# Loading the input norm's weights by themselves, and casting the first two weight pieces in halves

## The chip, the cores and the metric

The kernel runs on one core of a Trainium2 chip. The metric is the device time of one execution in microseconds (us). Before the change the median of three runs is 1170.52 us (1168.86 to 1172.1).

Engines are named as in the profile: PE is the matrix engine (PEld its weight loads), DVE the vector engine, ACT the scalar engine, POOL the general engine, SP the engine that issues most DMAs. A name with q (SPq, ACTq) is the issuing side of an engine. L12 is line 12 of the kernel's file.

## The reference, cut to what matters

One decoder layer on 256 tokens of width 2048, in float32:

```python
h = rms_norm(x, attn_norm_g)          # x * rsqrt(mean(x*x)) * attn_norm_g
proj = h @ w_in                       # 2048 x 4448
shifted = token_shift(proj[..., :RWKV_SHIFT_DIM], rwkv_mu)
y = concat(rwkv7_mixer(split(shifted), ...), mla_mixer(split(proj rest), ...))
x = x + y @ w_out
h = rms_norm(x, ffn_norm_g)
x = x + (silu(causal_conv3(h @ w_gate) + conv_b) * (h @ w_up)) @ w_down
return rms_norm(x, final_norm_g)
```

The change touches only how `x * attn_norm_g` and the first columns of `w_in` get onto the chip.

## The kernel before, in words

Every product is made of float32r halves: a value is split into `hi` (the value rounded by a cast) and `lo` (what the rounding lost), and a product is three matmuls, hi·hi, hi·lo and lo·hi. Weights come in pieces of 128 partitions x 1024 floats (512 KB). `piece` (L125) issues one DMA on SP into one of three `raw` buffers (`NRAW` is 3), casts it to `hi` on ACT (L133) and subtracts on DVE for `lo` (L134). A `raw` buffer comes free when its `lo` is done, so SP, which issues in order, waits there, and everything behind waits too.

The input is loaded transposed, in four tiles `xT` of 128 x 1024 (four 128-row blocks of 256 tokens each). `xsplit` (L137) multiplies each block by its 128 norm weights, held as one column per block, with ACT for `hi` (L143) and DVE for `lo` (L144). The norm's own factor, one over the root mean square of a token, is applied behind the product; its sums come from a second, token-major copy of `x` (tiles `xt`, L323, squared and summed on ACT, L324).

All per-channel vectors of the layer are packed in one array `vec` (128 x 283): its first 16 columns are the weights of the input norm, the other 267 are shift factors, decay offsets, convolution weights and the like. A second array `cst` (128 x 388) holds an identity, masks and the rope frequencies. Both are loaded from ACT's queue, `vec` at L122 before anything else, `cst` at L330, which stands behind the third input tile in the code and ends up at the head of ACT's queue.

The start runs as follows. PE does 20 matmuls of ones by ones (L297 and L298, each recorded as two passes), which depend on nothing but a memset. In the meantime SP loads xT tile 0, the first half of column tile 0 (`win[0, 0]`, rows 0 to 1023 of the input product), the first half of column tile 25, xT tiles 1 and 2, the second halves of column tiles 0 and 25, and xT tile 3. The loop at L327 then makes both column tiles together, four blocks at a time. After them come the positions (`rposi`, L338), column tile 26, two `xt` tiles, column tile 1, two more `xt` tiles, column tiles 2 and 3, and all the others.

What sets the order: on SP the code order is kept by hand; on the other engines a scheduler orders the instructions by its own estimate of when their data come. Every engine then works strictly in that order. From the end of the input projection on, PE's order is a list written out by hand.

Of the kernel before, what the change touches and what calls it, by code (L numbers as in the profile page):

```python
# [9 lines left out]
F32 = mybir.dt.float32  # L10
F32R = mybir.dt.float32r
BF16 = mybir.dt.bfloat16  # L12
I32 = mybir.dt.int32
AF = mybir.ActivationFunctionType
ALU = mybir.AluOpType
AX = mybir.AxisListType

P = 128
# [36 lines left out]
def hybrid_layer(ctx: ExitStack, tc: tile.TileContext, a: dict, out: bass.AP):  # L55
    nc = tc.nc
    V, S, PE = nc.vector, nc.scalar, nc.tensor
    PSUM = bass.MemoryType.PSUM

    sb = ctx.enter_context(tc.tile_pool(name="sb", bufs=1))  # L60
# [5 lines left out]
    def nm(s):  # L66
        uid[0] += 1
        return f"{s}{uid[0]}"

    NT2, NAT, NS4, NRAW, NHI, NLO, NMM, NCH, NT1 = 3, 2, 21, 3, 3, 3, 3, 3, 5  # L70

    def s4(dt=F32, n="s4"):
        return sb.tile([P, 1024], dt, tag="s4", name=nm(n), bufs=NS4)
# [8 lines left out]
    def hl4(slot, n, off=0):  # L82
        return a8(slot, n, off=off).rearrange("p (k s) t -> p k s t", s=2)
# [19 lines left out]
    def con(shape, n, dt=F32):  # L103
        return sb.tile(shape, dt, name=n, bufs=1)
# [3 lines left out]
    xT = a["xT"]  # L108
    xs_ = [hl4(g, "x") for g in range(4)]
    pad2 = con([P, 24], "pad2")  # L110
    nc.gpsimd.memset(pad2, 0.0)
    vec = con([P, NVEC], "vec")
    cst = con([P, NCST], "cst")

    def vv(name, i, rows=slice(0, P)):
        return vec[rows, VOFF[name] + i:VOFF[name] + i + 1]
# [2 lines left out]
    gmask = cst[:, C_MK:C_MK + P]  # L119
    blk2 = cst[:, C_BLK:C_BLK + 2]  # L120

    nc.scalar.dma_start(vec, a["vec"])  # L122


    def piece(src, dst=None, off=0):  # L125
        raw = sb.tile([P, 1024], F32, tag="raw", name=nm("raw"), bufs=NRAW)
        last_w[0] = nc.sync.dma_start(raw, src).ins
        if dst is None:
            hi = sb.tile([P, 1088], F32R, tag="hi", name=nm("hi"), bufs=NHI)[:, off:off + 1024]
            lo = sb.tile([P, 1088], F32R, tag="lo", name=nm("lo"), bufs=NLO)[:, off:off + 1024]  # L130
        else:
            hi, lo = (dst.rearrange("p k t -> p (k t)")[:, q * 1024:(q + 1) * 1024] for q in range(2))
        S.copy(hi, raw)  # L133
        last_lo[0] = V.tensor_tensor(lo, raw, hi.bitcast(F32), ALU.subtract).ins  # L134
        return hi, lo

    def xsplit(g):  # L137
        raw = s4(n="xraw").rearrange("p (k t) -> p k t", k=4)
        nc.sync.dma_start(raw, xT[:, g * 4:(g + 1) * 4, :])
        for j in range(4):  # L140
            k = g * 4 + j
            h = xs_[g][:, j, 0, :]
            S.activation(h, raw[:, j, :], AF.Copy, scale=vv("ag", k))  # L143
            last_x[0] = V.scalar_tensor_tensor(xs_[g][:, j, 1, :], raw[:, j, :], vv("ag", k),  # L144
                                               h.bitcast(F32), ALU.mult, ALU.subtract).ins
        return raw

    last_w, last_lo, last_x = [None], [None], [None]
# [11 lines left out]
    def prod_c(acc, pieces, act, kt0, n, first, last):  # L160
        hi, lo = pieces
        for j in range(n):
            for s in range(2):
                PE.matmul(acc[:, :T], hi[:, j * P:(j + 1) * P], act(kt0 + j)[:, s, :],  # L164
                          start=first and j == 0 and s == 0, stop=False)
        for j in range(n):
            i = PE.matmul(acc[:, :T], lo[:, j * P:(j + 1) * P], act(kt0 + j)[:, 0, :], start=False,  # L167
                          stop=last and j == n - 1)
        return i.ins
# [24 lines left out]
    def in_tile(i, pf=mm):  # L194
        acc = pf()
        for h in range(2):
            prod_c(acc, piece(a["win"][i, h]), x_hl, h * 8, 8, h == 0, h == 1)
        flush()
        return acc

    def rsqrt(src, scale, eps, w, eng=None, part=None):

        e = eng or nc.gpsimd
        m, y, t = st("rm", w), st("ry", w), st("rt", w)
        if part is None:
            e.tensor_scalar(m, src, 0.5 * scale, 0.5 * eps, ALU.mult, ALU.add)
        else:
            e.tensor_scalar(part, part, 0.5 * scale, 0.5 * eps, ALU.mult, ALU.add)
            e.tensor_scalar(m, src, 0.5 * scale, part, ALU.mult, ALU.add)
        e.tensor_scalar(y.bitcast(I32), m.bitcast(I32), -0.5, float(0x5f3759df - 2 ** 22 - 2 ** 31), ALU.mult, ALU.add)  # L210
        for _ in range(3):
            if e is V and w == 1:
                V.scalar_tensor_tensor(t, y, m, y, ALU.mult, ALU.mult)
            else:
                e.tensor_tensor(t, y, y, ALU.mult)
                e.tensor_tensor(t, t, m, ALU.mult)
            if e is V:
                V.scalar_tensor_tensor(y, t, -1.5, y, ALU.add, ALU.mult)
            else:
                e.tensor_scalar(t, t, -1.5, None, ALU.add)  # L220
                e.tensor_tensor(y, y, t, ALU.mult)
        return y


    def bcast(rs, dst, pf=ch, tf=t1):
        pb = pf("rsb")
        for tb in range(2):
            dg = tf("dg", P)
            V.tensor_scalar(dg, ident, rs[:, tb:tb + 1], None, ALU.mult)
            PE.matmul(pb[:, tb * P:(tb + 1) * P], ones, dg, start=True, stop=True)  # L230
        return V.tensor_copy(dst, pb[:, :T]).ins
# [83 lines left out]
    pcs = {}  # L315
    wt0 = (0, 25, 26)
    ssx = st("ssx", 4)
    kacc = {}

    def sums(h):  # L320
        for tb in range(2):
            t, o = s4(n="xt"), h * 2 + tb
            nc.sync.dma_start(t, a["x"][tb * P:(tb + 1) * P, h * 1024:(h + 1) * 1024])  # L323
            S.activation(t, t, AF.Square, accum_out=ssx[:, o:o + 1])  # L324

    with tc.manual_schedule(engines={mybir.EngineType.SP}):
        for g in range(4):  # L327
            xsplit(g)
            if g == 2:
                nc.scalar.dma_start(cst, a["cst"])  # L330
            if g % 2 == 0:
                for i in range(2):
                    pcs[i, g // 2] = piece(a["win"][wt0[i], g // 2])
            for i in range(2):
                hl = tuple(u[:, (g % 2) * 512:(g % 2 + 1) * 512] for u in pcs[i, g // 2])
                prod_c(acc0[i], hl, x_hl, g * 4, 4, g == 0, g == 3)
        posi = s4(n="rposi")[:, 0:T]
        nc.sync.dma_start(posi.bitcast(I32), a["pos"].broadcast_to([P, T]))  # L338
        for h in range(2):
            prod_c(acc0[2], piece(a["win"][26, h]), x_hl, h * 8, 8, h == 0, h == 1)  # L340
        sums(0)
        kacc[0] = in_tile(1)
        dve0 = last_lo[0]
        sums(1)
        kacc[1] = in_tile(2, at)
        rsB = sb.tile([P, T], F32, tag="rsB", name="rsB", bufs=1)
        nc.gpsimd.tensor_tensor(ssx[:, 0:2], ssx[:, 0:2], ssx[:, 2:4], ALU.add)
        rs1 = con([P, 2], "rs1")
        nc.gpsimd.tensor_copy(rs1, rsqrt(ssx[:, 0:2], 1.0 / DM, EPS, 2))
        bcast(rs1, rsB)  # L350
        kacc[2] = in_tile(3, ch)
        rope_tables()
        lora = s4(n="lora")
        nc.sync.dma_start(lora, a["lora"])
# [26 lines left out]
    def shifted(acc, i, rows=slice(0, P), dst=None):  # L381
        h = hbuf()[:, 1:258]
        scaled(h[rows, 1:257], acc, rsB, rows)
        o = t1("sh") if dst is None else dst
        S.activation(o[rows], h[rows, 1:257], AF.Copy, scale=om_mu[rows, i:i + 1])
        V.scalar_tensor_tensor(o[rows], h[rows, 0:256], vv("mu", i, rows), o[rows], ALU.mult, ALU.add)
        return o
# [74 lines left out]
    for p in range(8):  # L462
        pp, g = p // 2, p % 2
# [4 lines left out]
        k = shifted(acc, 1 + p)  # L468
# [44 lines left out]
    for p in range(8):  # L513
        pp, g = p // 2, p % 2
# [261 lines left out]
    bufs = {}  # L776
# [390 lines left out]
    for blk, nf in enumerate(NFS):  # L1167
# [11 lines left out]
        n = nf // 2  # L1179
        held = []  # L1180
        for c in range(4):
            accs = [mm() for _ in range(2)]
            for i in range(n - (4 if blk == 1 and c == 3 else 0)):
                prod_a(accs, piece(a["wdn"][c, f0 // 2 + i]), h_hi, h_lo, i * 2, 2, i == 0, i == n - 1)
                if blk == 1 and i == 2:
                    q = n - 4 + c
# [98 lines left out]
```

## Time and profile before

| | us |
|---|---|
| three runs, median (lowest to highest) | 1170.52 (1168.86 to 1172.1) |
| profiled execution, its own time | 1171.28 |
| span of its trace, first to last instruction | 1169.3 |
| PE busy | 1151.5 (98%) |
| DVE busy | 807.0 (69%) |
| ACT busy | 610.0 (52%) |

The profile's page covers one execution. Busy times are unions of instruction times; a matmul's recorded time includes its passage through the array, so that a PE shown as busy can still be streaming slower than it could. The idle time before an instruction is listed with what released it.

### The profile page before, as it was taken

What the parts mean: (1) busy time and instruction counts of PE and PEld (TensorE: products, weight loads), DVE (VectorE), ACT (ScalarE), POOL (GpSimd) and SP (SyncE); (2) the same over time, 40 slices, a digit from 0 to 9 for tenths busy, and PEclk for the clock granted to TensorE, in tenths of its full rate; (3) what the DMA queues carried; (4) which work ended last, traced back from release to release, by engine and by line L of the source; (5) the groups of instructions that cost most, each with busy time, mean ns of one, the idle gap of its engine ahead of it and who ended that gap; (6) DMA issues with size and microseconds to landing.
All of it is one profiled execution on the core that took longest, in us unless ns stands there. A gap on an engine that the chain in (4) does not pass through costs nothing.

```text
span 1169.3 us, 19472 instructions
## 1 busy us (share of the span) xinstructions
PE 1151.5 (98%) x7669; PEld 1018.2 (87%) x7669; DVE 807.0 (69%) x1333; ACT 610.0 (52%) x912; POOL 18.5 (2%) x45
## 2 busy tenths in 40 slices
PE   9999999999999999999999999999999999999996
PEld 9899999999878888888888888888888888888885
DVE  6897669746997577777767774544677777775653
ACT  6884346445653465555555553333455555554441
POOL 1200000000000000000000000000000000000000
PEclk9999999999999999999999999999999999999999
DMA  9645456715635555555555655665555565576672
GB/s 329 198 142 166 136 166 199 216 46 163 194 126 178 193 175 175 197 184 196 194 191 192 197 189 190 197 190 192 195 198 190 189 198 185 194 234 199 209 216 79
DMA packets 71227, 216.24 MB, mean 185 GB/s; under 512 B 17648, under 2 KB 18032, under 8 KB 71136
## 3 DMA queue, kind: packets, MB, share of 16 engines
q1 hardware_dynamic: 70208, 212.89, 56.2%
q10 hardware_dynamic: 576, 1.39, 0.4%
q8 instruction: 60, 0.98, 0.4%
q0 software_dynamic: 352, 0.72, 0.3%
q14 instruction: 31, 0.25, 0.1%
HBM read 210.85 MB, written 3.41 MB: 183 GB/s over the span
## 4 chain that ended last, share of the span: by engine, by line
PE 88%; DMA 4%; DVE 3%; ACT 2%; issue 1%; SPq 1%; ACTq 0%; DVEq 0%
PE mm L1080 27%; PE mm L1091 14%; PE mm L808 8%; PE mm L189 7%; PE mm L187 7%; PE mm L188 7%; PE mm L164 5%; PE mm L793 3%; PE mm L167 3%; PE mm L867 2%; DVE lo L134 1%; PE px L686 1%; PE pg L542 1%; DMA raw<-in_win 1%; PE py L686 1%
## 5 line engine op out<-in xcount | busy, mean ns | idle before, releaser
L134 DVE TENSOR_TENSOR lo<-raw,hi 128x1024 fp32r<-128x1024 f32 x376 | 459.8, 1223 | 269.2 <-ACT hi L133 198.9
L133 ACT CAST hi<-raw 128x1024 fp32r<-128x1024 f32 x376 | 395.7, 1053 | 422.5 <-PE mm L1080 126.1
L1080 PE MATMUL mm<-z,hi 128*128 128x512 f32 x1408 | 351.7, 392 | 0.8 <-DVE z L1032 0.8
L1080 PEld LDWEIGHTS mm<-z,hi 128*128 128x128 f32 x1408 | 251.5, 188 | 44.3 <-DVE z L1032 1.2
L1091 PEld LDWEIGHTS mm<-z,lo 128*128 128x128 f32 x1408 | 186.4, 188 | 14.9
L1091 PE MATMUL mm<-z,lo 128*128 128x256 f32 x1408 | 189.1, 276 | 0.0
L189 PE MATMUL mm<-hi,hl 128*128 128x512 f32 x336 | 130.7, 389 | 0.0
L188 PE MATMUL mm<-lo,hh 128*128 128x512 f32 x336 | 130.7, 389 | 0.0
L187 PE MATMUL mm<-hi,hh 128*128 128x512 f32 x336 | 119.7, 389 | 0.0
L164 PE MATMUL mm<-x,hi 128*128 128x256 f32 x768 | 103.0, 282 | 0.2 <-ACT hi L133 0.2
L164 PEld LDWEIGHTS mm<-x,hi 128*128 128x128 f32 x768 | 93.8, 188 | 2.0 <-ACT hi L133 0.4
L189 PEld LDWEIGHTS mm<-hi,hl 128*128 128x128 f32 x336 | 63.1, 188 | 13.2
L188 PEld LDWEIGHTS mm<-lo,hh 128*128 128x128 f32 x336 | 63.1, 188 | 13.1
L187 PEld LDWEIGHTS mm<-hi,hh 128*128 128x128 f32 x336 | 63.0, 188 | 12.9
L167 PE MATMUL mm<-x,lo 128*128 128x256 f32 x384 | 55.3, 281 | 0.0
L808 PE MATMUL mm<-hi,yhi 128*128 128x512 f32 x128 | 50.7, 396 | 0.0
L808 PE MATMUL mm<-lo,yhi 128*128 128x512 f32 x128 | 50.5, 395 | 0.0
L808 PE MATMUL mm<-hi,ylo 128*128 128x512 f32 x128 | 50.3, 393 | 0.0
L167 PEld LDWEIGHTS mm<-x,lo 128*128 128x128 f32 x384 | 48.8, 188 | 1.1 <-issue 1.0
L793 PE MATMUL mm<-x,hi 128*128 128x256 f32 x256 | 34.6, 286 | 0.0
L793 PEld LDWEIGHTS mm<-x,hi 128*128 128x128 f32 x256 | 31.6, 192 | 0.7
L808 PEld LDWEIGHTS mm<-hi,ylo 128*128 128x128 f32 x128 | 24.1, 188 | 5.3 <-DVE ylo L965 0.4
(294 smaller groups left out, 1120.6 us busy)
## 6 DMA issues: line engine op xcount, KB each, us to landing
raw<-in_wgu SPq DMA_DIRECT2D x176, 512.0 KB, 3.3
raw<-in_wdn SPq DMA_DIRECT2D x88, 512.0 KB, 4.2
raw<-in_win SPq DMA_DIRECT2D x70, 512.0 KB, 3.9
raw<-in_wout SPq DMA_DIRECT2D x32, 512.0 KB, 3.3
raw<-in_wuq SPq DMA_DIRECT2D x6, 512.0 KB, 4.4
xraw<-in_xT SPq DMA_DIRECT2D x4, 512.0 KB, 6.1
xt<-in_x SPq DMA_DIRECT2D x4, 512.0 KB, 7.5
raw<-in_wuv SPq DMA_DIRECT2D x4, 512.0 KB, 4.8
```

What stands on the lines that cost most here:

```text
L133: S.copy(hi, raw)
L134: last_lo[0] = V.tensor_tensor(lo, raw, hi.bitcast(F32), ALU.subtract).ins
L164: PE.matmul(acc[:, :T], hi[:, j * P:(j + 1) * P], act(kt0 + j)[:, s, :], start=first and j == 0 and s == 0, stop=False)
L167: i = PE.matmul(acc[:, :T], lo[:, j * P:(j + 1) * P], act(kt0 + j)[:, 0, :], start=False, stop=last and j == n - 1)
L187: PE.matmul(accs[tb], ah, wh, start=first and j == 0, stop=False)
L188: PE.matmul(accs[tb], ah, wl, start=False, stop=False)
L189: i = PE.matmul(accs[tb], al, wh, start=False, stop=last and j == n - 1)
L686: PE.matmul(dst[HS[h], a_ * 64:(a_ + 1) * 64], lhsT, rhs, start=begin and a_ == 0, stop=True, skip_group_check=True)
L793: PE.matmul(acc[:, :T], w[:, j * P:(j + 1) * P], act(j)[:, s, :], start=first and m == 0, stop=last and m == len(ops) - 1)
L808: PE.matmul(accs[tb], act, w, start=first and j == 0 and act is ah and w is wh, stop=last and j == 1 and act is al)
L1080: PE.matmul(accs[i], pcs[p][0][:, j * P:(j + 1) * P], z_hl(h * 8 + j), start=i not in seen, stop=False, skip_group_check=True)
L1091: PE.matmul(accs[i][:, :T], lo[:, j * P:(j + 1) * P], z_hl(h * 8 + j)[:, 0, :], start=False, stop=last and j == 7, skip_group_check=True)
```

## The change

The 16 norm columns get a tile of their own, `agt`, loaded from ACT's queue first (8 KB). The whole of `vec` (these 16 columns too, again) and `cst` are loaded from SP's queue, behind the positions. The scalar operands of L143 and L144 come from `agt`. For xT tile 0 and the first halves of column tiles 0 and 25, `first_parts` replaces `xsplit` and `piece`: the same DMAs in the same order, but the two weight pieces are cast and subtracted 512 columns at a time, and the order on ACT and DVE is written out: input blocks 0 and 1, first half of tile 0's piece, input blocks 2 and 3, first half of tile 25's piece, then the two second halves.

```diff
-    nc.scalar.dma_start(vec, a["vec"])
+    agt = con([P, 16], "agt")
+    nc.scalar.dma_start(agt, a["vec"][:, 0:16])
...
-            S.activation(h, raw[:, j, :], AF.Copy, scale=vv("ag", k))
-            last_x[0] = V.scalar_tensor_tensor(xs_[g][:, j, 1, :], raw[:, j, :], vv("ag", k),
+            S.activation(h, raw[:, j, :], AF.Copy, scale=agt[:, k:k + 1])
+            last_x[0] = V.scalar_tensor_tensor(xs_[g][:, j, 1, :], raw[:, j, :], agt[:, k:k + 1],
...
+    def first_parts():
+
+        engines = {mybir.EngineType.SP, mybir.EngineType.Activation, mybir.EngineType.DVE}
+        xr = s4(n="xraw").rearrange("p (k t) -> p k t", k=4)
+        nc.sync.dma_start(xr, xT[:, 0:4, :])
+        w = []
+        for i in range(2):
+            w.append([sb.tile([P, 1024], F32, tag="raw", name=nm("raw"), bufs=NRAW)]
+                     + [sb.tile([P, 1088], F32R, tag=t, name=nm(t), bufs=NHI)[:, 0:1024] for t in ("hi", "lo")])
+            nc.sync.dma_start(w[i][0], a["win"][wt0[i], 0])
+            pcs[i, 0] = tuple(w[i][1:])
+
+        def x_part(k):
+            h = xs_[0][:, k, 0, :]
+            S.activation(h, xr[:, k, :], AF.Copy, scale=agt[:, k:k + 1])
+            V.scalar_tensor_tensor(xs_[0][:, k, 1, :], xr[:, k, :], agt[:, k:k + 1], h.bitcast(F32), ALU.mult, ALU.subtract)
+
+        def w_part(i, q):
+            raw, hi, lo = (u[:, q * 512:(q + 1) * 512] for u in w[i])
+            S.copy(hi, raw)
+            V.tensor_tensor(lo, raw, hi.bitcast(F32), ALU.subtract)
+
+        with tc.manual_schedule(engines=engines):
+            x_part(0)
+            x_part(1)
+            w_part(0, 0)
+            x_part(2)
+            x_part(3)
+            w_part(1, 0)
+            w_part(0, 1)
+            w_part(1, 1)
+
...
     with tc.manual_schedule(engines={mybir.EngineType.SP}):
+        first_parts()
         for g in range(4):
-            xsplit(g)
+            if g:
+                xsplit(g)
             if g == 2:
-                nc.scalar.dma_start(cst, a["cst"])
-            if g % 2 == 0:
                 for i in range(2):
                     pcs[i, g // 2] = piece(a["win"][wt0[i], g // 2])
...
         nc.sync.dma_start(posi.bitcast(I32), a["pos"].broadcast_to([P, T]))
+        nc.sync.dma_start(vec, a["vec"])
+        nc.sync.dma_start(cst, a["cst"])
```

Where the instructions stand, in three places. Numbers behind a name tell buffers apart. First ACT at the head of the program, before (x_65 to x_68 are the four split input tiles, hi_126 and hi_132 the first halves of column tiles 0 and 25):

```order
L122 DMA vec<-in_vec 128x283
L313 ACT_TABLE_LOAD
L313 ACTIVATE warm_106<-ones 128x2
L330 DMA cst<-in_cst 128x388
L143 ACTIVATE x_65<-xraw_114,vec 128x256 x4
L133 CAST hi_126<-raw_124 128x1024
L133 CAST hi_132<-raw_130 128x1024
L143 ACTIVATE x_66<-xraw_160,vec 128x256 x4
L143 ACTIVATE x_67<-xraw_194,vec 128x256 x4
L133 CAST hi_207<-raw_205 128x1024
```

and now (hi_118 and hi_122 are those first halves):

```order
L123 DMA agt<-in_vec 128x16
L314 ACT_TABLE_LOAD
L314 ACTIVATE warm_107<-ones 128x2
L335 ACTIVATE x_65<-xraw_115,agt 128x256 x2
L340 CAST hi_118<-raw_117 128x512
L335 ACTIVATE x_65<-xraw_115,agt 128x256 x2
L340 CAST hi_122<-raw_121 128x512
L340 CAST hi_118<-raw_117 128x512
L340 CAST hi_122<-raw_121 128x512
L144 ACTIVATE x_66<-xraw_168,agt 128x256 x4
L144 ACTIVATE x_67<-xraw_202,agt 128x256 x4
L134 CAST hi_214<-raw_212 128x1024
```

One DMA is shorter, one has left, two casts have become four, and the first of them has moved between the input blocks. DVE's subtractions follow the same pattern.

Second SP from the seventh DMA on, before (raw_211 is the second half of column tile 25, xraw_241 xT tile 3, raw_277 and raw_307 the two halves of column tile 26):

```order
L127 DMA raw_211<-in_win 128x1024
L139 DMA xraw_241<-in_xT 128x1024
L338 DMA rposi_275<-in_pos 128x256
L127 DMA raw_277<-in_win 128x1024
L127 DMA raw_307<-in_win 128x1024
L323 DMA xt_337<-in_x 128x1024
```

and now:

```order
L128 DMA raw_218<-in_win 128x1024
L140 DMA xraw_248<-in_xT 128x1024
L371 DMA rposi_282<-in_pos 128x256
L372 DMA vec<-in_vec 128x283
L373 DMA cst<-in_cst 128x388
L128 DMA raw_286<-in_win 128x1024
L128 DMA raw_316<-in_win 128x1024
L356 DMA xt_346<-in_x 128x1024
```

Two DMAs have come in ahead of column tile 26.

Third PE at its head, before (mm_108 and mm_109 accumulate column tiles 0 and 25):

```order
L298 MATMUL wps_78<-ones 128x128 x20
L164 MATMUL mm_108<-x_65,hi_126 128x256 x8
L167 MATMUL mm_108<-x_65,lo_127 128x256 x4
L164 MATMUL mm_109<-x_65,hi_132 128x256 x8
L164 MATMUL mm_108<-x_66,hi_126 128x256
L167 MATMUL mm_109<-x_65,lo_133 128x256 x4
```

and now:

```order
L299 MATMUL wps_79<-ones 128x128 x20
L165 MATMUL mm_109<-x_65,hi_118 128x256 x7
L165 MATMUL mm_110<-x_65,hi_122 128x256 x7
L165 MATMUL mm_109<-x_65,hi_118 128x256
L168 MATMUL mm_109<-x_65,lo_119 128x256 x4
L165 MATMUL mm_110<-x_65,hi_122 128x256
L168 MATMUL mm_110<-x_65,lo_123 128x256 x4
```

The 20 matmuls of ones still stand first, and the second column tile's matmuls have moved ahead of the `lo` products. Behind the input tiles every engine's order is as before.

## The prediction

> **What bounds the kernel now.** I read the page first, then the busy time by stage, then the instructions of the first 26 us in order of time, because the change ends there: behind the fourth input tile no engine's order differs.
>
> ```profile
> PE 1151.5 (98%) x7669; PEld 1018.2 (87%) x7669; DVE 807.0 (69%) x1333; ACT 610.0 (52%) x912; POOL 18.5 (2%) x45
> PE 88%; DMA 4%; DVE 3%; ACT 2%; issue 1%; SPq 1%; ACTq 0%; DVEq 0%
> ```
>
> PE is the chain for 88% of the span, so a microsecond won at the start reaches the end only if PE gets ahead and stays ahead. The stages (columns: window, its length, busy time and instructions of PE, PEld, DVE, ACT, POOL, granted clock, share of the DMA engines, GB/s):
>
> ```profile
> 1.10:6.40 5.30, 5.30 (x25) 5.30 (x26) 0.80 (x2) 2.83 (x6) 2.69 (x7) 1.00 0.86 293
> 6.55:8.10 1.55, 1.55 (x16) 1.55 (x15) 1.10 (x3) 1.25 (x3) 0.00 (x0) 1.00 1.02 418
> 8.10:25.06 16.96, 16.96 (x147) 16.96 (x145) 14.23 (x26) 12.76 (x22) 0.00 (x0) 1.00 0.96 343
> 25.06:25.56 0.50, 0.28 (x3) 0.07 (x1) 0.02 (x1) 0.45 (x1) 0.00 (x0) 1.00 0.84 270
> 50.00:70.00 20.00, 19.62 (x145) 16.91 (x144) 19.76 (x48) 18.65 (x39) 0.00 (x0) 1.00 0.34 106
> ```
>
> Up to 8.1 us PE does its matmuls of ones: about 0.21 us a pass in the first row, 0.10 in the second (5.30/25, 1.55/16). Then come 16.96 us with 145 weight loads, 0.118 us each and no hole, while the DMA engines are 96% busy. At 25.06 PE stops for 0.50 us. From 50 to 70 DVE is full. The instructions behind this (start, length, what; in brackets the idle time before and what ended it):
>
> ```profile
> 1.09 7.09 PEld L298 LDWEIGHTS wps<-ones 128*128 128x128 f32 x40 [1.09 <-POOL ones L295]
> 5.06 1.71 ACT L143 ACTIVATE x<-xraw,vec 128x256 fp32r<-128x256 f32 x4 [2.37 <-DMA vec<-in_vec]
> 6.67 1.03 ACT L133 CAST hi<-raw 128x1024 fp32r<-128x1024 f32 x1
> 7.73 2.58 DVE L134 TENSOR_TENSOR lo<-raw,hi 128x1024 fp32r<-128x1024 f32 x2 [0.45 <-ACT hi L133]
> 8.00 1.05 ACT L133 CAST hi<-raw 128x1024 fp32r<-128x1024 f32 x1 [0.30 <-DMA raw<-in_win]
> 8.11 1.01 PEld L164 LDWEIGHTS mm<-x,hi 128*128 128x128 f32 x8
> 9.28 3.31 ACT L143 ACTIVATE x<-xraw,vec 128x256 fp32r<-128x256 f32 x8 [0.23 <-DMA xraw<-in_xT]
> 12.50 1.98 ACT L133 CAST hi<-raw 128x1024 fp32r<-128x1024 f32 x2
> 24.46 1.05 ACT L133 CAST hi<-raw 128x1024 fp32r<-128x1024 f32 x1 [0.23 <-PE at L164]
> 25.56 1.90 PEld L164 LDWEIGHTS mm<-x,hi 128*128 128x128 f32 x16 [0.43 <-ACT hi L133]
> ```
>
> ACT does wait for `vec`, 2.37 us, and the change shortens that. But PE does not wait for ACT: the first weight half is cast at 7.70 (6.67 + 1.03), and PE's first product at 8.11 stands right behind the ones, which end with their last load at 8.18 (1.09 + 7.09), with no idle time listed. **The start is set by the 20 matmuls of ones, and these stay.**
>
> What ends the stage is a load. The chain of waits within the first 45 us:
>
> ```profile
> 2.12 7.13 DMA xraw<-in_xT
> 9.26 0.02 issue
> 9.28 3.31 ACT x L143 x8
> ...
> 17.19 7.17 DMA raw<-in_win
> 24.36 0.02 issue
> ```
>
> The load issued at 17.19 is the first half of column tile 1. It lands at 24.36, its cast runs to 25.51, and PE goes on at 25.56. A 512 KB load takes 7.17 us there because others lie ahead of it: it is bound by how fast the queue drains.
>
> **The change, part by part.** PE's needs first, from the rows above: product n of the stage starts at 8.11 + 0.118 n. The second halves of tiles 0 and 25 are wanted at 13.8 (n = 48), tile 26 at 19.4 (n = 96), tile 1 at 25.1 (n = 144). None moves earlier, since 8.11 stays.
>
> *Loads.* `vec` and `cst` leave the front. What they cost there (per queue, 1.7 to 6.5 us: packets, MB, share of the 16 engines; then KB and us from issue to landing):
>
> ```profile
> q10 hardware_dynamic: 284, 0.34, 23.1%
> vec<-in_vec ACTq DMA_DIRECT2D x1, 141.5 KB, 4.3
> cst<-in_cst ACTq DMA_DIRECT2D x1, 194.0 KB, 5.8
> xraw<-in_xT SPq DMA_DIRECT2D x1, 512.0 KB, 4.1
> dL<-G SPq DMA_DIRECT2D x32, 16.0 KB, 1.9
> ```
>
> 23.1% of 4.8 us is 1.11 us of each engine. `agt` takes back between nothing and `vec`'s part of that, 0.47 (1.11 x 141.5/335.5); a sixteenth of the bytes in as many rows, I take 0.25. So the first six loads of SP land some 0.85 us earlier (0.64 to 1.11). `agt` itself lands between 2.6 us (issued at 0.74 like `vec`, with the 1.9 of a 16 KB transfer) and `vec`'s 5.06; as it has the same 128 rows to pass among the rows of xT tile 0, I take 4.6. The tile itself, issued at 0.75 and landing 4.1 later, at 4.85, comes to 4.0 to 4.2.
>
> The Trainium skill, "DMA: Bandwidth & Descriptors", section "Issuing engines are not separate DMA queues", says that DMAs issued from ACT and SP run on the same 16 engines and interleave, so the issuing queue buys nothing. By it the move alters the order of the bytes and not the time at which all of them are in, and the sum would hold zero for everything behind `cst`; that `vec` and xT tile 0 overlapped in q10 and q1 agrees.
>
> Behind `cst` the 1.11 us are paid again. For the load that ends the stage the bytes ahead of it are the same plus 8 KB: zero, to +0.25. One thing may be saved: a thin stretch.
>
> ```profile
> 16.10:16.70 0.60, 0.60 (x8) 0.60 (x6) 0.60 (x3) 0.00 (x0) 0.00 (x0) 1.00 0.63 178
> 16.77 1.05 ACT L133 CAST hi<-raw 128x1024 fp32r<-128x1024 f32 x1 [0.68 <-DVE x L144]
> 19.41 1.96 PEld L164 LDWEIGHTS at<-x,hi 128*128 128x128 f32 x16
> 21.56 0.35 DVE L257 TENSOR_SCALAR rw<-rw,cst 128x256 f32<-128x256 f32 x1
> ```
>
> There the queue ran nearly dry, at 0.63 of the engines' time, 0.22 us lost. With `vec` and `cst` in the queue it is full at that point: -0.22. A new dry spot can open earlier, below: 0 to +0.22.
>
> *Column tile 26* lands by about 16.7 now and is cast at 16.77; it goes to 16.7 - 0.85 + 1.11, some 17.0. PE wants it at 19.41, less 1.05 for the cast is 18.36. The tile's slack covers the two transfers; without it each 0.1 us would be paid in full. `cst` is first read at 21.56, `vec` later: both land near 16. SP's two extra issues (0.4 each) lie ahead of tile 26, whose data wait for the queue anyway.
>
> *Casts in halves.* Prices of 512 columns:
>
> ```profile
> 56.25 0.61 ACT L431 ACTIVATE pi<-tw 128x512 f32<-128x512 f32 x1
> 49.97 0.42 DVE L400 TENSOR_TENSOR sglo<-sh,sghi 128x256 fp32r<-128x256 f32 x1
> 8.99 0.33 SPq L127 DMA_DIRECT2D raw<-in_win  x1
> ```
>
> ACT pays four times 0.61 for 2.08, +0.36; DVE between 0.42 and 1.22 a half, I take 0.7, four for 2.58, +0.2. ACT used to idle 0.30 and 0.23 us here, and the walk is: blocks 0 and 1 from 4.6; tile 0's piece, landing about 5.8, first half to 6.4; blocks 2 and 3 to 7.3; tile 25's piece lands near 7.1 (7.98 now), so three half casts from 7.3 to 9.1. The next input blocks start at 9.1, not 9.28: 0.2 earlier, or 0.6 later if the head start were nothing (8.0 + 3 x 0.61 = 9.8). The second half of tile 0 is then cast by 13.3, before 13.5 (12.50 + half of 1.98), wanted at 13.8: free, or 0.3 of stall at the late end.
>
> *The new wait.* The seventh load of SP takes over tile 0's buffer, which came free after its single subtraction (issue at 8.99). Now its second half must be subtracted too, as DVE's seventh instruction: cast by 8.5, subtracted by 9.3 behind the half of tile 25, issue 9.3, late end 10.0. Queued behind it are xT tile 3, the positions, `vec`, `cst` and everything else. The six loads ahead drain by about 10.5, so the queue stays full or goes thin once, 0.22 at the price of the row above.
>
> *Sum.* PE's start 0; DMA order 0; thin stretch -0.22; new thin stretch half of +0.22, rounded 0; casts 0. That is -0.2 us of the profiled execution's 1171.28 (span 1169.3, 1.98 around it): 1171.1. The median of the runs lies 0.76 under that execution: 1170.52 - 0.2, **1170.3 us**. The ends of the unknown costs: -0.85 (the head start lasts) to +0.8 (0.3 + 0.22 + 0.25).
>
> **Rivals.** *The head start lasts.* If every load up to tile 1 and the `xt` tiles came 0.85 us earlier, the 0.50 us hole at 25.06 would close, and the row norm behind them would come earlier too.
>
> ```profile
> 36.76 0.48 DVE L229 TENSOR_SCALAR dg<-cst,rs 128x128 f32<-128x128 f32 x2 [2.32 <-POOL rs L349]
> ```
>
> DVE waits 2.32 us there on the chain that starts with those `xt` tiles, and then fills up to 70 us. All of it moves by 0.85 at most: 1169.7. Against it: the bytes are the same.
>
> *Small rows clog SP's queue.* Behind the positions, which are 1 KB rows, throughput was low:
>
> ```profile
> rposi<-in_pos SPq DMA_DIRECT2D x1, 128.0 KB, 5.5
> 8.10:13.00 4.90, 4.90 (x44) 4.90 (x43) 4.78 (x10) 4.67 (x10) 0.00 (x0) 1.00 1.03 413
> 13.00:16.10 3.10, 3.10 (x28) 3.10 (x28) 3.01 (x5) 3.09 (x6) 0.00 (x0) 1.00 0.98 305
> ```
>
> 3.10 x (1 - 305/413) is 0.81 us lost for 128 KB. `vec` and `cst` are 335.5 KB in rows of 1.1 and 1.5 KB: 2.1 us lost if they did the same. Tile 26 then lands near 18.8, past 18.36, and tile 1, which has no slack, 2.1 later: +2.1, 1172.6, slower than before. It decides as soon as the loss exceeds the 0.22 saved. Against it: in q10 the same rows cost 1.11 us in all.
>
> *The clock window.*
>
> ```profile
> 231.70:238.60 6.90, 6.90 (x116) 6.38 (x111) 1.51 (x3) 2.70 (x5) 0.00 (x0) 0.51 0.40 154
> ```
>
> One stretch runs at half clock, behind many tiny matmuls and a wait. It costs 6.9 x 0.49 = 3.4 us. If a shift of half a microsecond moved it off, 1166.9; if a second came, 1173.7. Nothing in the start speaks for either: the granted clock is 1.00 in every row up to 25 us. The Trainium skill, "TensorE: Matmul & The Clock Gate", section "What's actually happening", has the gate watch free-running windows, so the same work can meet it differently from run to run; by it this would come in either kernel, and one trace cannot show it.
>
> **How the numbers follow.** The forecast 0.70, the lasting head start 0.15, the clogged queue 0.08, the clock 0.05 (half to each side), something not seen 0.02. A difference of 0.3% (3.5 us), about what a measurement of this kernel can tell from no change, is reached by none of these prices alone; the clock comes within 0.1 of it, and the scatter of the runs (1168.86 to 1172.1) can carry it over. So faster 0.03, slower 0.03, same 0.94. The cases lie between 1169.7 and 1172.6, a median of few runs moves by some 1.5: 1167.7 to 1172.8.
>
> **What would show it.** Right: the first input block on ACT starts between 4.0 and 5.06; PE's first product stays at the end of the ones, 8.1 or wherever they end; the seventh load is issued after 8.99; tile 26 is cast after 16.77 without PE waiting; the hole before tile 1 is between 0 and 0.8 us, and PE's products keep 0.118 us. Wrong: PE's first product well before the ones used to end, a hole at 13.8 or 19.4, or an end that moves by more than 1.5 us without a change of the half-clock stretch.

## The result, and the profile after

The changed kernel takes 1183.57 us (median of five runs, 1182.66 to 1185.99) against 1170.05 us of the kernel before (five runs, 1168.86 to 1172.1): a ratio of 1.0119, 95% interval 1.0107 to 1.0131. It is **13.5 us slower**, where 1170.3 was forecast. The profiled execution of the changed kernel took 1182.66 us with a span of 1180.6, 11.3 longer than before.

First the two lines of the page that open the prediction, now of the changed kernel:

```profile
PE 1164.1 (99%) x7669; PEld 1030.1 (87%) x7669; DVE 808.2 (68%) x1335; ACT 610.7 (52%) x914; POOL 18.2 (2%) x45
PE 91%; DMA 3%; DVE 2%; ACT 2%; issue 1%; SPq 0%; ACTq 0%; DVEq 0%
```

The same 7669 matmul records keep PE busy for 12.6 us more (1164.1 against 1151.5), and PE's share of the chain has risen. DVE gained 1.2 us and ACT 0.7. So the time did not go into a wait: PE itself takes longer over the same work.

Which work, the groups of instructions by line and shape tell (busy us, mean ns of one, idle before). Before:

```profile
L1080 PE MATMUL mm<-z,hi 128*128 128x512 f32 x1408 | 351.7, 392 | 0.8 <-DVE z L1032 0.8
L1091 PE MATMUL mm<-z,lo 128*128 128x256 f32 x1408 | 189.1, 276 | 0.0
L187 PE MATMUL mm<-hi,hh 128*128 128x512 f32 x336 | 119.7, 389 | 0.0
L164 PE MATMUL mm<-x,hi 128*128 128x256 f32 x768 | 103.0, 282 | 0.2 <-ACT hi L133 0.2
L167 PE MATMUL mm<-x,lo 128*128 128x256 f32 x384 | 55.3, 281 | 0.0
L793 PE MATMUL mm<-x,hi 128*128 128x256 f32 x256 | 34.6, 286 | 0.0
```

and after (line numbers are 1 or 35 higher):

```profile
L1115 PE MATMUL mm<-z,hi 128*128 128x512 f32 x1408 | 353.2, 392 | 0.8 <-DVE z L1067 0.8
L1126 PE MATMUL mm<-z,lo 128*128 128x256 f32 x1408 | 196.3, 282 | 0.0
L188 PE MATMUL mm<-hi,hh 128*128 128x512 f32 x336 | 119.7, 389 | 0.0
L165 PE MATMUL mm<-x,hi 128*128 128x256 f32 x768 | 105.2, 285 | 0.0
L168 PE MATMUL mm<-x,lo 128*128 128x256 f32 x384 | 56.4, 284 | 0.0
L828 PE MATMUL mm<-x,hi 128*128 128x256 f32 x256 | 35.6, 290 | 0.0
```

The products of weights with `z` (the gate and up projections) and with `x` (the input projection) are longer: +7.2, +1.5, +2.2, +1.1 and +1.0, together 13.0 us. (A group's busy time also counts where its neighbours overlap it, so the groups add up to a little more than the 12.6 us of PE as a whole.) Per product that is 5.1 ns for z,lo (7.2 us / 1408) and 2.9 ns for x,hi (2.2 / 768). The down projection's group (hi,hh) is the same to the tenth. The products with `z` begin more than 400 us behind the change. They come in the same order and with the same data as before.

It can be seen in stretches without any hole too. Windows of equal length inside one stage, the gate and up projections and then the first down projection (window, length, busy time and count of PE, PEld, DVE, ACT, POOL, granted clock, DMA share, GB/s). Before:

```profile
460.00:680.00 220.00, 220.00 (x1284) 193.58 (x1283) 160.32 (x241) 124.44 (x182) 0.00 (x0) 1.00 0.59 193
735.00:810.00 75.00, 75.00 (x333) 62.10 (x332) 36.02 (x32) 29.07 (x28) 0.00 (x0) 1.00 0.60 192
```

After, 5 and 7 us later:

```profile
465.00:685.00 220.00, 220.00 (x1261) 193.54 (x1260) 157.35 (x236) 121.91 (x177) 0.00 (x0) 1.00 0.58 189
742.00:817.00 75.00, 75.00 (x332) 62.13 (x331) 36.19 (x32) 28.73 (x28) 0.00 (x0) 1.00 0.61 193
```

Clock 1.00 and no idle time in all four. In 220 us PE does 23 products fewer (220/1284 is 171.3 ns, 220/1261 is 174.5); in the down projection the pace has not changed. DVE, ACT and the DMA engines do less in the first window because they follow PE.

If each instruction of PE is compared with itself in the other trace, the changed kernel lags by 1.2 us at 34 us, 0.6 at 68, 4.2 at 228 (input projection), 2.4 at 442, 7.15 at 700, an unchanged 7.15 through the first down projection to 817, 11.05 at 1060, the same at 1100, and 11.4 at the last product. From 68 us on nearly all of its growth lies where `x` or `z` streams. The drop behind 228 us has a cause of its own, the half-clock stretch of the prediction. Before and after:

```profile
222.00:252.00 30.00, 29.25 (x699) 0.89 0.42 104
```

```profile
222.00:252.00 30.00, 29.54 (x693) 0.94 0.56 142
```

(window, length, PE's busy time, granted clock, DMA share, GB/s). It cost 30 x 0.11 = 3.3 us before and 30 x 0.06 = 1.8 after, 1.5 of the 1.8 us by which the lag falls there.

The start, where the change was made, reads as follows after it; first ACT, then PE's weight loads, then SP's issues, all by time (start, length, what; idle time before):

```profile
4.99 0.91 ACT L335 ACTIVATE x<-xraw,agt 128x256 fp32r<-128x256 f32 x2 [2.30 <-DMA agt<-in_vec]
...
7.42 1.64 ACT L340 CAST hi<-raw 128x512 fp32r<-128x512 f32 x3
8.96 3.30 ACT L144 ACTIVATE x<-xraw,agt 128x256 fp32r<-128x256 f32 x8
...
19.65 1.05 ACT L134 CAST hi<-raw 128x1024 fp32r<-128x1024 f32 x1 [3.62 <-PE mm L165]
...
24.74 1.05 ACT L134 CAST hi<-raw 128x1024 fp32r<-128x1024 f32 x1 [0.20 <-DMA raw<-in_win]
```

```profile
1.09 7.43 PEld L299 LDWEIGHTS wps<-ones 128*128 128x128 f32 x40 [1.09 <-POOL ones L296]
8.44 1.84 PEld L165 LDWEIGHTS mm<-x,hi 128*128 128x128 f32 x15
...
20.75 1.95 PEld L165 LDWEIGHTS at<-x,hi 128*128 128x128 f32 x16 [0.86 <-ACT hi L134]
...
26.43 1.73 PEld L165 LDWEIGHTS mm<-x,hi 128*128 128x128 f32 x14
```

```profile
3.21 6.56 SPq L128 DMA_DIRECT2D raw<-in_win  x2
...
11.77 3.05 SPq L128 DMA_DIRECT2D raw<-in_win  x2
```

The hole before column tile 1 (0.50 us at 25.06 before) is gone, and a hole of 0.86 us before column tile 26 has come. What the start leaves behind, a lag of 0.6 us at 68 us, is well under a microsecond. The prediction dealt with this part; the 13 us are elsewhere.

### The profile page after: what moved, and what is told of

It reads as the page before. It is cut to its first block, busy times and chain, and to the rows that moved or that the text cites. A ratio compares the mean times of both kernels' runs of the same rounds, so it can differ in the third digit from the quotient of the medians.

```text
span 1180.6 us, 19478 instructions
## 1 busy us (share of the span) xinstructions
PE 1164.1 (99%) x7669; PEld 1030.1 (87%) x7669; DVE 808.2 (68%) x1335; ACT 610.7 (52%) x914; POOL 18.2 (2%) x45
## 4 chain that ended last, share of the span: by engine, by line
PE 91%; DMA 3%; DVE 2%; ACT 2%; issue 1%; SPq 0%; ACTq 0%; DVEq 0%
PE mm L1115 27%; PE mm L1126 14%; PE mm L843 8%; PE mm L188 7%; PE mm L190 7%; PE mm L189 7%; PE mm L165 7%; PE mm L828 3%; PE mm L168 3%; DMA raw<-in_win 2%; PE mm L902 2%; PE pg L577 1%; PE px L721 1%; PE py L721 1%; DVE lo L135 1%
## 5 line engine op out<-in xcount | busy, mean ns | idle before, releaser
L1115 PEld LDWEIGHTS mm<-z,hi 128*128 128x128 f32 x1408 | 253.3, 189 | 46.2 <-DVE z L1067 1.2
L1126 PEld LDWEIGHTS mm<-z,lo 128*128 128x128 f32 x1408 | 192.1, 190 | 13.9
L1126 PE MATMUL mm<-z,lo 128*128 128x256 f32 x1408 | 196.3, 282 | 0.0
L165 PE MATMUL mm<-x,hi 128*128 128x256 f32 x768 | 105.2, 285 | 0.0
L165 PEld LDWEIGHTS mm<-x,hi 128*128 128x128 f32 x768 | 95.8, 188 | 1.6 <-issue 0.3
L828 PE MATMUL mm<-x,hi 128*128 128x256 f32 x256 | 35.6, 290 | 0.0
L828 PEld LDWEIGHTS mm<-x,hi 128*128 128x128 f32 x256 | 32.4, 192 | 0.7
```

What stands on the lines that cost most here:

```text
L828: PE.matmul(acc[:, :T], w[:, j * P:(j + 1) * P], act(j)[:, s, :], start=first and m == 0, stop=last and m == len(ops) - 1)
L1115: PE.matmul(accs[i], pcs[p][0][:, j * P:(j + 1) * P], z_hl(h * 8 + j), start=i not in seen, stop=False, skip_group_check=True)
L1126: PE.matmul(accs[i][:, :T], lo[:, j * P:(j + 1) * P], z_hl(h * 8 + j)[:, 0, :], start=False, stop=last and j == 7, skip_group_check=True)
```

## The experiments

**Theories.** *Addresses*: `agt` is a new tile of 64 bytes per partition, allocated behind `cst`. SBUF space is given out in the order in which tiles are first asked for, so everything allocated behind it (raw, hi, lo and the work tiles) lies 64 bytes higher, while the input tiles, allocated ahead of `vec`, stay. The built program lists the operands' addresses, and they agree: what changed is the distance between the weights that PE loads and the tile that it streams. *Rival 1*: the start (loads and halves) shifts the phase of DMA, DVE and PE against each other and makes all later stages slower. *Rival 2*: any move of the addresses, or of the DMA's targets, costs, and not the distance.

The kernel had two tiles that nothing reads, `pad` (8 columns ahead of the input tiles) and `pad2` (24 columns behind them). They make the test cheap: they can be resized without touching any instruction that matters.

**Addresses held.** The change in full, with `agt` taking 16 of the 24 columns of `pad2`, so that every other tile lies where it lay before:

```diff
-    pad2 = con([P, 24], "pad2")
+    pad2 = con([P, 8], "pad2")
     nc.gpsimd.memset(pad2, 0.0)
+    agt = con([P, 16], "agt")
     vec = con([P, NVEC], "vec")
     cst = con([P, NCST], "cst")
...
-    agt = con([P, 16], "agt")
```

> The changed kernel with its 16-column tile put into the room of an unused 96-byte filler ahead of the vectors, so that every tile behind it stands at the address it had before the change. Placement theory (the 64 bytes of the new tile moved the weight buffers against the input tiles, and that made PE's 256-column products slower): 1170.6 us, 1169.5 to 1172, products of the feed-forward part 113.3 ns apart as before. Rival (loads, waits or halved casts cost it): 1183, products 118.6 apart as in the changed kernel.

1170.84 us, ratio 1.0011 (1.0002 to 1.0020) to the kernel before. The groups:

```profile
L1126 PE MATMUL mm<-z,lo 128*128 128x256 f32 x1408 | 189.1, 276 | 0.0
L165 PE MATMUL mm<-x,hi 128*128 128x256 f32 x768 | 102.7, 282 | 0.0
```

The kernel before took 1169.7 us in the runs beside it. With the same loads, casts and order as the changed kernel, the loss is 1.1 us in place of 13.5. Rival 1 falls.

The expectation's 113.3 and 118.6 ns are from the start of one product to the start of the next. In the traces the median of these steps within a run of z,lo products is 113 ns before, 120 with the change and 113 here. The busy time per product in the table below is longer, because in each run of eight the last product counts with the whole of its recorded length.

**64 bytes and nothing else.** The kernel before, with an unused tile where the change has `agt`:

```diff
     cst = con([P, NCST], "cst")
+    pad3 = con([P, 16], "pad3")
...
+    nc.gpsimd.memset(pad3, 0.0)
```

> The kernel before with nothing but an unused 64-byte tile where the changed kernel has its new one; no load, wait or cast differs. Placement theory: 1182 to 1184, products 118.6 ns apart. Rival: 1170, 113.3 apart.

1184.13 us, ratio 1.0120 (1.0106 to 1.0134): the whole loss of the change, without any part of it that does something.

```profile
L1082 PE MATMUL mm<-z,hi 128*128 128x512 f32 x1408 | 353.2, 392 | 0.8 <-DVE z L1034 0.8
L1093 PE MATMUL mm<-z,lo 128*128 128x256 f32 x1408 | 196.3, 282 | 0.0
```

The same two numbers as in the changed kernel.

**All tiles moved together.** The kernel before with 64 bytes more ahead of the input tiles; every address changes, no distance between these tiles does:

```diff
-    pad = con([P, 8], "pad")
+    pad = con([P, 24], "pad")
```

> The kernel before with a filler ahead of the input tiles longer by 64 bytes, so that input tiles, vectors and weight buffers all move by 64 and their distances stay. Placement theory in the form that the distance between weights and moving operand counts: 1170, 113.3 ns. In the form that the address of the weight buffers counts: 1183, 118.6 ns.

1170.25 us, ratio 1.0004 (0.9994 to 1.0013).

```profile
L1091 PE MATMUL mm<-z,lo 128*128 128x256 f32 x1408 | 189.1, 276 | 0.0
```

Rival 2 falls: it is the distance.

**The input tiles alone moved by 64.** `pad` larger and `pad2` smaller by the same 16 columns; the weights and everything behind stay:

```diff
-    pad = con([P, 8], "pad")
+    pad = con([P, 24], "pad")
...
-    pad2 = con([P, 24], "pad2")
+    pad2 = con([P, 8], "pad2")
```

> The kernel before with the input tiles alone moved up by 64 bytes (one filler longer, the next shorter), weight buffers where they were. If the distance counts: the distance falls from 64 to 0 modulo 256, the distance that the latent products have, whose products are 113 to 120 ns apart in both kernels; a change of time either way, 1165 to 1184. If the address of the weight buffers counts: 1170.

1188.34 us, ratio 1.0155 (1.0141 to 1.0169), slower still.

```profile
L1080 PE MATMUL mm<-z,hi 128*128 128x512 f32 x1408 | 356.6, 395 | 0.8 <-DVE z L1032 0.8
L1091 PE MATMUL mm<-z,lo 128*128 128x256 f32 x1408 | 196.0, 282 | 0.0
L164 PE MATMUL mm<-x,hi 128*128 128x256 f32 x768 | 106.1, 286 | 0.4 <-ACT hi L133 0.4
```

**Other distances, and the period.** `pad3` with 32 and with 8 columns (weights up by 128 and by 32), `pad` and `pad2` both 16 (input tiles up by 32), `pad3` with 64 columns (weights up by 256):

```diff
+    pad3 = con([P, 32], "pad3")
...
+    pad3 = con([P, 8], "pad3")
...
-    pad = con([P, 8], "pad")
+    pad = con([P, 16], "pad")
-    pad2 = con([P, 24], "pad2")
+    pad2 = con([P, 16], "pad2")
...
+    pad3 = con([P, 64], "pad3")
```

> The kernel before with an unused tile of 128 bytes at the place: distance from input tiles to weight buffers 192 modulo 256 (64 in the kernel before, 128 with the change, 0 in the kernel with the input tiles moved). If only the pairing of odd and even multiples of 64 counts, 192 is as good as 64: 1170, 113 to 115 ns. If the fast place is 64 alone: 1183 to 1188, 118 to 120 ns.

1181.47 us, ratio 1.0089 (1.0072 to 1.0106). Neither forecast was met: the 256-column products are almost as fast as before, but z,hi alone is 5.3 us longer (357.0 against 351.7).

> As before with an unused tile of 32 bytes: distance 96. If addresses count in lines of 64 bytes, one of the two operands straddles lines differently and the time lies between those of 64 and 128, 1170 to 1184; if the distance counts smoothly, about 1177; if 64 to 127 is one class, 1170.

1184.62 us, ratio 1.0120 (1.0105 to 1.0135), the slow end of the first forecast; a smooth rule (1177) and one class from 64 to 127 (1170) do not hold.

> As before with the input tiles alone moved up by 32 bytes: distance 32. Smooth: about 1179, half way from 1170 (64) to 1188 (0). In classes of 64: as 0, 1188.

1187.81 us, ratio 1.0151 (1.0136 to 1.0167). This is the time forecast for classes of 64, a reading that the kernel before this one does not bear out.

> The kernel before with an unused tile of 256 bytes: distance from input tiles to weight buffers 320, which is 64 modulo 256. If the rule has a period of 256: 1170 and 113 to 115 ns between products. If only the one distance of the kernel before is fast, or the period is longer: 1181 to 1188.

1169.92 us, ratio 1.0003 (0.9994 to 1.0012): 256 bytes cost nothing, 32, 64 and 128 do. With 256 bytes z,hi and z,lo are at 351.7 and 189.1 again; z,hi of the kernel with 128 bytes:

```profile
L1082 PE MATMUL mm<-z,hi 128*128 128x512 f32 x1408 | 357.0, 395 | 0.8 <-DVE z L1034 0.8
```

All of them in one table. The expectations counted the distance between the buffers of weights and of `x`. The operands of the built program show more: the streamed part of `z` starts 128 bytes further within its 256 than that of `x`. So the table has both, as the address of the loaded weights less that of the streamed tile, modulo 256; next to them busy ns per product (a group's busy time over its count).

| kernel | weights − x | x,hi ns | weights − z | z,lo ns | z,hi ns | median us |
|---|---|---|---|---|---|---|
| before | 64 | 134.1 | 192 | 134.3 | 249.8 | 1170 |
| all moved by 64 | 64 | 133.7 | 192 | 134.3 | 249.8 | 1170.25 |
| weights + 256 | 64 | 134.0 | 192 | 134.3 | 249.8 | 1169.92 |
| weights + 32 | 96 | 136.7 | 224 | 137.4 | 254.2 | 1184.62 |
| weights + 64 | 128 | 137.1 | 0 | 139.4 | 250.9 | 1184.13 |
| the change | 128 | 137.0 | 0 | 139.4 | 250.9 | 1183.57 |
| weights + 128 | 192 | 135.8 | 64 | 135.7 | 253.6 | 1181.47 |
| x + 64 | 0 | 138.2 | 128 | 139.2 | 253.3 | 1188.34 |
| x + 32 | 32 | 136.7 | 160 | 140.1 | 253.9 | 1187.81 |

For the 256-column products 64 and 192 are the two best distances, and all the others tried are slower. Which of 64 and 192 is better differs between `x` and `z`. For 512 columns 192 is the best and 0 the next best, while 64 is slow. The rule behind it is not settled by these runs, and a move of all tiles together was tried by 64 bytes alone.

**The latent and hidden tiles.** `x` and the weights 64 higher, the work tiles that hold the latents `cl` and the gated hidden units `hh`, `hl` left where they were:

```diff
-    pad = con([P, 8], "pad")
+    pad = con([P, 24], "pad")
...
-    pad2 = con([P, 24], "pad2")
+    pad2 = con([P, 8], "pad2")
...
+    pad3 = con([P, 16], "pad3")
+    nc.gpsimd.memset(pad3, 0.0)
```

> The kernel before with input tiles and weight buffers moved up by 64 bytes together, while the buffers between them (the latent tiles and the gated products) stay: distance to the input tiles 64 as before, distance of weights to latent tiles and gated products 64 in place of 0. If the rule found for the input tiles holds there too, the 384 products of the latents gain 2 ns each (0.8 us) and the 1008 products of the down projection something if they follow it: 1165 to 1169.5. If it is a matter of the 256-column products on input tiles alone: 1170.

1173.46 us, ratio 1.0028 (1.0017 to 1.0039), slower by 3.3 us. The groups with `z` stay; those of the down projection and of `cl` do not. In this kernel:

```profile
L188 PE MATMUL mm<-lo,hh 128*128 128x512 f32 x336 | 131.6, 392 | 0.0
L189 PE MATMUL mm<-hi,hl 128*128 128x512 f32 x336 | 131.3, 391 | 0.0
L187 PE MATMUL mm<-hi,hh 128*128 128x512 f32 x336 | 120.9, 393 | 0.0
L869 PE MATMUL mm<-cl,hi 128*128 128x256 f32 x160 | 23.1, 285 | 0.5 <-ACT qn L859 0.5
L869 PE MATMUL mm<-cl,lo 128*128 128x256 f32 x80 | 13.3, 289 | 0.0
```

and before:

```profile
L189 PE MATMUL mm<-hi,hl 128*128 128x512 f32 x336 | 130.7, 389 | 0.0
L188 PE MATMUL mm<-lo,hh 128*128 128x512 f32 x336 | 130.7, 389 | 0.0
...
L867 PE MATMUL mm<-cl,hi 128*128 128x256 f32 x160 | 22.6, 282 | 0.5 <-ACT qn L857 0.5
L867 PE MATMUL mm<-cl,lo 128*128 128x256 f32 x80 | 13.1, 286 | 0.0
```

+0.9, +0.6, +1.2, +0.5 and +0.2 are 3.4 us, against 3.3 measured. The expectation, a gain or nothing, was missed. The expectation went by the buffers, and took the distance of both kinds as 0 before. By the operands, the weights of `cl` start 64 bytes into their buffer, so `cl` went from 64 to 128: +3.1 ns a product, as with `x` on the same step (+2.9). In the down projection the roles are turned: the hidden tile is loaded and the weights stream, 512 columns at a time. Loaded less streamed went from 0 to 192, for 2 to 4 ns a product. Of this pair only these two distances were tried.

**The direct effect, apart.** Three kernels with all addresses as before. First the changed kernel with held addresses and `vec` and `cst` behind column tile 26 instead of ahead of it:

```diff
-        nc.sync.dma_start(vec, a["vec"])
-        nc.sync.dma_start(cst, a["cst"])
...                                          # column tile 26, both halves
+        nc.sync.dma_start(vec, a["vec"])
+        nc.sync.dma_start(cst, a["cst"])
```

> The changed kernel at the addresses of before, with the vectors and constants on SP's queue behind both halves of column tile 26 and not ahead of them. If those two transfers are what makes PE wait about 1.7 us for tile 26, the hole near 19 us falls to 0.3 or less and a hole before tile 1 (near 25 us) of up to 1 us comes in its place; the time falls by 0 to 1 us against the changed kernel at those addresses, 1169.5 to 1171.

1170.76 us, ratio 1.0006 (0.9997 to 1.0015). The hole before tile 26 goes, one before tile 1 takes its place:

```profile
19.00 1.95 PEld L165 LDWEIGHTS at<-x,hi 128*128 128x128 f32 x16
...
26.38 1.72 PEld L165 LDWEIGHTS mm<-x,hi 128*128 128x128 f32 x14 [1.66 <-ACT hi L134]
```

The wait moves and the time stays, 1170.76 us against 1170.84 with the two loads ahead of tile 26. Tile 1's cast starts 0.4 us later here (25.28 against 24.90). The rest of the 1.66 us, more than the 1 us expected, is that PE, not held up at tile 26, comes to tile 1 earlier. The program built from this edit differs in more than the two loads: behind PE's 260th of 7024 instructions the scheduler ordered part of the input projection anew. The rows above stand ahead of that, but the time at the end is not that of the two loads alone.

Next the loads alone (no halves), with held addresses:

```diff
-        first_parts()
         for g in range(4):
-            if g:
-                xsplit(g)
-            if g == 2:
+            xsplit(g)
+            if g % 2 == 0:
```

> The loads of the change alone (norm weights first, vectors and constants on SP's queue ahead of column tile 26), pieces cast whole, at the addresses of before. If the loads make the hole before tile 26, it is here too, 0.8 to 1.8 us near 19 us. Time 1169.5 to 1171.5.

1170.27 us, ratio 1.0007 (0.9998 to 1.0016).

```profile
19.89 1.95 PEld L165 LDWEIGHTS at<-x,hi 128*128 128x128 f32 x16 [1.14 <-ACT hi L134]
```

PE waits 1.14 us before tile 26, as expected. The next kernel, with the halves alone, has no such wait, so the hole belongs to the loads.

And the halves alone: the kernel before with `first_parts` of the change, scaled from `vec`, and with `vec` and `cst` on ACT's queue as before:

```diff
         for g in range(4):
-            xsplit(g)
+            if g:
+                xsplit(g)
...
+            S.activation(h, xr[:, k, :], AF.Copy, scale=vv("ag", k))
```

> The halved casts alone, in their written order, with vectors and constants loaded from ACT's queue as in the kernel before, at its addresses. No hole before tile 26 if the loads make it; the buffer of tile 0 comes free later, issue of the seventh load near 9.8 rather than 9.0. Time 1169.5 to 1171.

1172.47 us, ratio 1.0020 (1.0009 to 1.0030): alone they cost 2.6 us (1.1 to 3.5), more than was expected.

```profile
19.91 1.91 PEld L164 LDWEIGHTS at<-x,hi 128*128 128x128 f32 x16
...
27.06 1.10 PEld L164 LDWEIGHTS mm<-x,hi 128*128 128x128 f32 x9 [1.62 <-ACT hi L133]
```

No hole before tile 26, as expected. Tile 1 starts 1.5 us later than before (27.06 against 25.56) behind a hole of 1.62. Held against the trace of before, product by product, this kernel is 2.2 us behind at 34 us and still at 150, so most of its loss comes from the start. The full change with held addresses is 1.0 us behind at 34 us, 0.1 at 100 and 0.3 ahead at the end. Why it catches up and the halves alone do not is open.

The 1.1 us that the full change with held addresses costs on the medians need not come from the start at all. The mean granted clock of that kernel's 11 runs is 0.9946, that of the 21 runs before beside it 0.9958. If the time follows the clock, 0.0012 of 1170 us is 1.4 us (an estimate). No kernel tried is faster than the one before.

## Why the prediction was wrong

**The step that failed** is the one that closed the case in its first paragraph: "the change ends there: behind the fourth input tile no engine's order differs". The order does not differ, but the addresses do. `agt` was costed as a load (0.25 us of the engines, 64 bytes a row) and at nothing as a tile. With that, "PE's products keep 0.118 us" was taken for granted and no rival was held against it. It was wrong for 1408 + 1408 products with `z` and some 1680 with `x`: 13.0 us by the groups, against a sum of -0.2. The 64-byte filler alone gives +14.4 us on the medians, the changed kernel with held addresses +1.1.

The range was not worked out from its own cases either: 1.5 us on both sides of 1169.7 to 1172.6 is 1168.2 to 1174.1, not 1167.7 to 1172.8. The 1183.57 us lie outside of both.

The sign was in the code: two tiles, `pad` and `pad2`, that only a memset ever touches. A filler that nothing reads has a size for some reason, and the change put 64 bytes beside it.

**The others, by their order.**

- *PE's start is set by the ones*: right. The ones end at 8.52 (1.09 + 7.43), the first product loads at 8.44 behind them, with no idle time. But it is right by the luck of these two traces. The ones took from 5.96 to 7.43 us over the 14 kernels traced. In five of the kernels that have the start of before and only other addresses, they ended so early that PE then waited for ACT's cast, for 0.17 to 0.87 us. The largest of these waits, of the kernel with the weights moved by 32 bytes:

```profile
1.09 5.96 PEld L299 LDWEIGHTS wps<-ones 128*128 128x128 f32 x40 [1.09 <-POOL ones L296]
7.92 1.01 PEld L165 LDWEIGHTS mm<-x,hi 128*128 128x128 f32 x8 [0.87 <-ACT hi L134]
```

  There `vec` did hold up PE, by way of ACT. The three other kernels that load `agt` first have short ones too (6.23 to 6.77 us), and none waits there: PE starts at 7.22 to 7.77 us. The head start is real when the ones are short; it was lost again in the waits before tiles 26 and 1.
- *`agt` lands at 4.6*: the first block started on it at 4.99, 0.07 us before it started on `vec`. Of its range, 2.6 to 5.06, the late end held; with the loads alone the block started at 4.64. The Trainium skill, "DMA: Bandwidth & Descriptors", section "Issuing engines are not separate DMA queues", has transfers of both queues interleave on the same engines; that an 8 KB load beside 512 KB loads is hardly sooner in than one of 141.5 KB (4.2 us from issue to landing against 4.3) agrees with it.
- *Casts in halves free, next input blocks at 9.1*: three half casts end at 9.06, the blocks start at 8.96, and there is no hole at 13.8: right in the changed kernel. With held addresses, where PE started 0.9 us earlier (7.54), there are holes of 0.22 and 0.16 us at 13.44 and 14.60, near the 0.3 of its late end.
- *Seventh load issued at 9.3 instead of 8.99*: the pair of issues that it ends finishes at 9.77 against 9.32, so +0.45 instead of +0.3, inside the late end.
- *Tile 26 covered by its slack*: wrong. Its cast came at 19.65, not some 0.3 us later than 16.77, and PE waited 0.86 us. This is the rival of the clogged queue, forecast at 18.8. The row names PE as releaser; in the kernel with held addresses the same cast waits about as long, the load ends it, and PE waits 1.68 us:

```profile
19.81 1.04 ACT L134 CAST hi<-raw 128x1024 fp32r<-128x1024 f32 x1 [3.38 <-DMA raw<-in_win]
```

  Time was lost in two thin stretches, one from the small rows' issue at 10.29 on, the other around and behind the end of SP's two issues of tile 26, which took 3.05 us from 11.77, 2.3 of them a wait for DVE's `lo` to free a `raw` buffer:

```profile
8.00:10.30 2.30, 2.30 (x22) 2.30 (x21) 2.30 (x5) 2.30 (x7) 0.00 (x0) 1.00 0.98 399
10.30:11.80 1.50, 1.50 (x15) 1.50 (x14) 1.50 (x5) 1.50 (x5) 0.00 (x0) 1.00 0.84 229
...
14.00:16.30 2.30, 2.30 (x22) 2.30 (x21) 2.30 (x4) 2.04 (x5) 0.00 (x0) 1.00 0.69 235
```

  Against 399 GB/s they lost 1.5 x (1 - 229/399) = 0.64 and 2.3 x (1 - 235/399) = 0.95 us. The rival's mechanism, little throughput behind small rows, fits the first stretch; for the second the reading, that SP's wait for a buffer left the queue thin, is argued from the order in time and not tested. Its weight of 0.08 was too small; but its end price of +2.1 did not come, since tile 1 was not late as well.
- *The hole before tile 1 stays between 0 and 0.8*: it went to 0. With the 0.86 us before tile 26 the two sides cancel nearly, as the sum of -0.2 had it for other reasons.
- *The clock stretch*: it did move, to the good side, by 1.5 of the 3.4 us allowed. But that is no effect of the change that could be shown. With held addresses the same 30 us gave 0.89, as before, and with the loads alone 1.00. Over 30 runs of the kernel before, the mean clock went from 0.993 to 0.998, and 0.003 of it is about this stretch, so one trace of each cannot tell the kernel from the run.

With held addresses the parts that were costed come to +1.1 us (0.2 to 2.3), inside the range. The terms of the sum were small, as forecast, though not right one by one: tile 26's slack did not cover the two transfers. The one that was left out, 12.4 us, was eleven times as large as all of them together.

## What to carry to other kernels

A tile added, removed or resized moves every tile allocated behind it, and in a kernel bound by PE the distance between loaded and streamed operand, modulo 256 bytes, can be worth more than a percent; compare the operands' addresses of both kernels before costing anything else. When a small edit at one end changes the pace of unchanged work elsewhere, look at the groups by shape first, and test with an unused tile of the same size: it separates the edit from its place in memory. Give a new tile the room of an old filler, or put it behind everything else, and keep fillers that nothing reads until it is known what they hold apart.

## What the runs showed of the hardware that was not expected

- The pace of back-to-back products depends on where the two operands lie against each other: z,lo took 134.3 ns at a distance of 192 and 139.4 at 0; x,hi 134.1 at 64 and 138.2 at 0. Moving all tiles by 64 bytes changes nothing (1170.25 us), nor does a distance larger by 256 (1169.92). The recorded length of a matmul shows it too (276 and 282 ns).
- The Trainium skill, "TensorE: Matmul & The Clock Gate", section "Step-by-step: what each phase is for", gives PE two independent read ports of SBUF and says that loading the next weights takes no read bandwidth from the running matmul. Read by itself, that sentence leaves no reason why the two addresses should matter to each other; here they do, by up to 5.8 ns in 134 (z,lo at 160). The page does not speak of addresses, and whether the two reads meet at a bank or something else does this, no run here shows.
- The matmuls of ones at the start, the same 40 weight loads in every kernel, took from 5.96 to 7.43 us. This does not follow the edit: the changed kernel took 7.43 and the same program with held addresses 6.55, the kernel before 7.09 and the same with its weights moved by 32 bytes 5.96. Each kernel has one trace, so whether it varies from run to run or with the addresses is open. It is as large as everything the change could have won there.
